# A linear-attention recurrence on one core: converting loads become plain ones, and the stores move to GpSimd's queue

## The chip, the core and the metric

The kernel runs on one core of a Trainium2 chip. The metric is device time in microseconds (us), the median of three runs. A core has five engines that run side by side: PE (TensorE, matrix products), DVE (VectorE), ACT (ScalarE), POOL (GpSimd) and SP (SyncE, which here only issues transfers). Sixteen DMA engines move data between HBM (main memory) and SBUF (the on-chip memory of 128 partitions). PSUM holds the results of PE.

## The reference

For each of 16 batches and each of 256 channels, a recurrence runs over 2048 time steps. It keeps a weighted sum of v (`aa`), the sum of the weights (`bb`) and a running maximum (`pp`) for safe exponentials:

```python
for t in range(seq_len):
    ww = u + k[t]
    qq = max(pp, ww)
    e1, e2 = exp(pp - qq), exp(ww - qq)
    output[t] = (e1 * aa + e2 * v[t]) / (e1 * bb + e2 + 1e-08)
    ww = pp - w + k[t]
    qq = max(ww, k[t])
    e1, e2 = exp(ww - qq), exp(k[t] - qq)
    aa, bb, pp = e1 * aa + e2 * v[t], e1 * bb + e2, qq
```

k, v and the output are float32 of 16 x 2048 x 256, 33.55 MB each.

## The kernel before

Time is cut into 16 chunks of 128 steps (`TC`), and each chunk into four parts of four batches. A part is a slot, numbered n from 0 to 63 (n = 4c + p). In slot n the kernel

- issues the loads of slot n + 6 (`load`), 512 KB of k and 512 KB of v, in rows of 1 KB
- takes exponentials of sums of k that PE made (`exps`, on ScalarE)
- rounds k(n + 2) to PE's format (`round_k`) and v(n + 1) to bf16 (`cast_v`), and multiplies by v (`times_v`), on VectorE
- makes the denominators of slot n - 10 (`den`, `recip`) and the numerators of slot n - 11 (`num`, `mult`), and stores slot n - 11

Between chunks a small chain (`state_...`, spread over slots by `plan`) carries the state: GpSimd and VectorE work on 128 x 32 tiles, and four small transfers (`inject`) put the state into the rows of the next chunk's operands.

Every instruction stands in program order on its engine (`K(...)` keeps it). A transfer is issued by an engine's queue in that order too: one that waits for its data or its buffer holds those behind it.

```python
    kpool = ctx.enter_context(tc.tile_pool(name="kpool", bufs=AHEAD))      # AHEAD = 6
    vpool = ctx.enter_context(tc.tile_pool(name="vpool", bufs=5))
    vbpool = ctx.enter_context(tc.tile_pool(name="vbpool", bufs=4))
    rpool = ctx.enter_context(tc.tile_pool(name="rpool", bufs=6))

    def v_mode(n):                                                         # LAG = 10
        return "dma" if n >= LAG and n % 4 == 3 else "dve"

    def load_v(n, queue=SP):
        if v_mode(n) == "dma":
            VB[n] = vbpool.tile([128, 4, Dm], BF16, tag="vb", name="vb")
            K(POOL.dma_start(out=VB[n], in_=rows_of(v, n)))                # float32 -> bf16 on the way
        else:
            vr_of[n] = vpool.tile([128, 4, Dm], F32, tag="vr", name="vr")
            K(queue.dma_start(out=vr_of[n], in_=rows_of(v, n)))
    # ... cut ...
    def round_k(n):
        # ... cut ...
        K(DVE.tensor_copy(km, kr_of.pop(n)))
    # ... cut ...
    def inject(c):
        # ... cut: cb is copied by VectorE ...
                K(POOL.dma_start(
                    out=EZR[r:r + 1, 2 * q, r0:r0 + 4, :, :].rearrange("o p i (b x) -> o (p i b) x", b=4),
                    in_=cb[x:x + 32, :]))

    def store(n):
        K(SP.dma_start(out=rows_of(out, n), in_=RD.pop(n).rearrange("p i (n d) -> p (i n) d", n=2)))
    # ... cut ...
    for n in range(LAG, NP):                       # NP = 64
        q, qp = n - LAG, n - LAG - 1
        load(n + AHEAD)
        if qp >= 0:
            num(qp, NUMB, 0)
        den(q)
        small_work(n, "nums")
        exps(n)
        small_work(n, "act")
        if qp >= 0:
            mult(qp, NUMB, 0)
        small_work(n, "mid")
        if n + 2 < NP:
            round_k(n + 2)
        if n + 1 < NP:
            cast_v(n + 1)
        # ... cut ...
        recip(q, lambda: small_work(n, "recip"))
        if qp >= 0:
            mult(qp, NUMB, 1)
        small_work(n, "scan")
        if qp >= 0:
            store(qp)
        if n + 1 < NP:
            times_v(n)
            small_work(n, "chain")
            logs(n + 1)
```

Of the kernel before, what the change touches and what calls it, by code (L numbers as in the profile page):

```python
# [7 lines left out]
F32 = mybir.dt.float32  # L8
F32R = mybir.dt.float32r
BF16 = mybir.dt.bfloat16  # L10
ALU = mybir.AluOpType
ACT = mybir.ActivationFunctionType
# [3 lines left out]
def kernel(  # L16
# [9 lines left out]
    K = tc.keep_in_program_order  # L26
    PE, DVE, SC, POOL, SP = nc.tensor, nc.vector, nc.scalar, nc.gpsimd, nc.sync

    B, T, Dm = k.shape
# [4 lines left out]
    NP = 4 * NST  # L34
    RING = 12
    AHEAD = 6
    LAG = 10
# [5 lines left out]
    kpool = ctx.enter_context(tc.tile_pool(name="kpool", bufs=AHEAD))  # L43
    vpool = ctx.enter_context(tc.tile_pool(name="vpool", bufs=5))
    vbpool = ctx.enter_context(tc.tile_pool(name="vbpool", bufs=4))
    rpool = ctx.enter_context(tc.tile_pool(name="rpool", bufs=6))
    small = ctx.enter_context(tc.tile_pool(name="small", bufs=2))
    tiny = ctx.enter_context(tc.tile_pool(name="tiny", bufs=1))
    ps = ctx.enter_context(tc.tile_pool(name="ps", bufs=1, space=bass.MemoryType.PSUM))
# [2 lines left out]
    kr_of, vr_of, VB = {}, {}, {}  # L52

    def v_mode(n):
        return "dma" if n >= LAG and n % 4 == 3 else "dve"

    def rows_of(x, n):
        c, p = divmod(n, 4)
        return x[4 * p:4 * p + 4, c * TC:(c + 1) * TC, :].rearrange("n t d -> t n d")

    def load_k(n, queue=SP):
        kr_of[n] = kpool.tile([128, 4, Dm], F32, tag="kr", name="kr")
        K(queue.dma_start(out=kr_of[n], in_=rows_of(k, n)))

    def load_v(n, queue=SP):
        if v_mode(n) == "dma":
            VB[n] = vbpool.tile([128, 4, Dm], BF16, tag="vb", name="vb")
            K(POOL.dma_start(out=VB[n], in_=rows_of(v, n)))
        else:
            vr_of[n] = vpool.tile([128, 4, Dm], F32, tag="vr", name="vr")  # L70
            K(queue.dma_start(out=vr_of[n], in_=rows_of(v, n)))


    def load(n):
        for x, f in ((n - 1, load_v), (n, load_k)) if n < LAG + AHEAD else ((n, load_k), (n, load_v)):
            if x < NP and (f == load_k or v_mode(x) != "dma"):
                f(x)

# [35 lines left out]
    for n in range(2, AHEAD):  # L116
        load_k(n)
        load_v(n - 1)
# [61 lines left out]
    def round_k(n):  # L180
        km = consts.tile([128, 4, Dm], F32R, tag=f"km{n % 2}", name="km") if n < 2 else KM[n - 2]
        K(DVE.tensor_copy(km, kr_of.pop(n)))  # L182
        KM[n] = km
# [21 lines left out]
    def exps(n):  # L205
        if n < TURNS:
            for q in range(2):
                K(SC.activation(ez(n)[:, q], half(n, q), ACT.Exp))  # L208
        else:
            K(SC.activation(ez(n)[:, 0:2], PS[:, 0:4, :].rearrange("p (q i) x -> p q i x", q=2), ACT.Exp))  # L210

    def cast_v(n):
        mode = v_mode(n)
        if mode == "dma":
            return
        vb = vbpool.tile([128, 4, Dm], BF16, tag="vb", name="vb")
        vr = vr_of.pop(n)
        if mode == "act":
            K(SC.activation(vb, vr, ACT.Copy))
        elif mode == "pool":  # L220
            K(POOL.tensor_copy(vb, vr))
        else:
            K(DVE.tensor_copy(vb, vr))  # L223
        VB[n] = vb

    def times_v(n):
        vb = VB.pop(n).rearrange("p (i n) d -> p i (n d)", i=2)
        K(DVE.tensor_mul(ez(n)[:, 2:4], ez(n)[:, 0:2], vb.unsqueeze(1).broadcast_to([128, 2, 2, D])))  # L228
# [94 lines left out]
    def state_next(c):  # L323
        G, tb = st.pop((c, "G")), st.pop((c, "tb"))
        AB, nxt = AB_of[c % 2], AB_of[(c + 1) % 2]
        y = tiny.tile([128, 2, 32], F32, tag="y", name="y")
        K(POOL.tensor_mul(y, AB[:, :, 1, :], G[:, 1, :].unsqueeze(1).broadcast_to([128, 2, 32])))
        K(POOL.tensor_add(nxt[:, :, 0, :], y, tb[:, :, 1, :]))

        if 4 * c + 11 < NP:  # L330
            load_v(4 * c + 11)


    def turn_back(c):
        t = MISC[:, Dm:Dm + 128]
# [17 lines left out]
    RD = {}  # L353

    def den(n):
        for m, q in (("L", 0), ("Id", 1)):
            for i in range(2):
                K(PE.matmul(DENB[:, i, :], mats[m], ez(n)[:, q, i, :], start=q == 0, stop=q == 1,  # L358
                            skip_group_check=True))
# [9 lines left out]
    def num(n, bank, i):  # L369
        for m, q in (("LN", 2), ("IdN", 3)):  # L370
            K(PE.matmul(bank, mats[m], ez(n)[:, q, i, :], start=q == 2, stop=q == 3, skip_group_check=True))  # L371

    def mult(n, bank, i):
        rd = RD[n]
        K(DVE.tensor_mul(rd[:, i, :], bank, rd[:, i, :]))  # L375

    def store(n):
        K(SP.dma_start(out=rows_of(out, n), in_=RD.pop(n).rearrange("p i (n d) -> p (i n) d", n=2)))

    def last_outputs(n, H):  # L380
        c, p = divmod(n, 4)
# [7 lines left out]
    for c in range(NST):  # L389
        s = 4 * c + 3  # L390
        plan = [(s + 1, "act" if s + 1 < LAG else "recip", copy_sums), (s + 1, "pe", turn),
                (s + 2, "act", state_logs), (s + 2, "mid", state_frames), (s + 2, "scan", state_scan), (s + 2, "scan", state_offsets),
                (s + 3, "recip", state_weights), (s + 3, "chain", state_chain),
                (s + 4, "nums", turn_back), (s + 4, "mid", inject), (s + 4, "mid", state_next)]
        if c == 0:
            plan = [(s + 1, "act", copy_sums), (s + 1, "pe", turn), (s + 2, "act", state_logs),
                    (s + 2, "chain", state_frames), (s + 2, "chain", state_scan), (s + 2, "chain", state_offsets),
                    (s + 3, "act", state_weights), (s + 3, "chain", state_chain),
                    (s + 4, "logs", turn_back), (s + 4, "logs", inject), (s + 4, "round", state_next)]
        if c == 1:  # L400
            plan = [(s + 1, "act", copy_sums), (s + 1, "pe", turn), (s + 2, "act", state_logs),
                    (s + 2, "chain", state_frames), (s + 2, "chain", state_scan), (s + 2, "chain", state_offsets)] + plan[6:]
        if c == NST - 1:
            plan = [(s + 1, "copy", copy_sums), (s + 1, "turn", turn),
                    (s + 1, "post", state_logs), (s + 1, "mid", state_frames), (s + 1, "mid", state_scan), (s + 1, "mid", state_offsets),
                    (s + 2, "post", state_weights), (s + 2, "first", state_chain),
                    (s + 3, "turn", turn_back), (s + 3, "first", inject)]
        for slot, where, f in plan:
            later.setdefault((slot, where), []).append((f, c))

    def small_work(n, where):
        for f, c in later.pop((n, where), []):
            f(c)
# [10 lines left out]
    logs(0)  # L424
    round_k(1)
    cast_v(0)
    for n in range(LAG):

# [19 lines left out]
    for n in range(LAG, NP):  # L448

        q, qp = n - LAG, n - LAG - 1  # L450
        load(n + AHEAD)
        if qp >= 0:
            num(qp, NUMB, 0)
        den(q)
# [13 lines that stand above are left out]
            num(qp, NUMB, 1)  # L468

        sums(n - 1)  # L470
        recip(q, lambda: small_work(n, "recip"))
        if qp >= 0:
            mult(qp, NUMB, 1)
        small_work(n, "scan")
        if qp >= 0:
            store(qp)
        if n + 1 < NP:
            times_v(n)
            small_work(n, "chain")
            logs(n + 1)  # L480
        else:
            den(q + 1)
        small_work(n, "pe")
    sums(NP - 1)
    small_work(NP, "copy")
    late = []
    for n in range(NP, NP + LAG + 1):

        q, qp = n - LAG, n - LAG - 1
        H = PS[:, 2 * (n % 2):2 * (n % 2) + 2, :]  # L490
        for i in range(2):
            num(qp, H[:, i, :], i)
        small_work(n, "turn")
        if q < NP:
            recip(q, lambda: small_work(n, "recip"))
        small_work(n, "post")
        if q + 1 < NP:
            den(q + 1)
        small_work(n, "first")
        if qp == NP - 1:  # L500
            last_outputs(qp, H)
            break
        late.append((qp, H))
        if n != NP + 1:

            for x, bank in late:
                mult(x, bank, slice(0, 2))
                store(x)
            late = []
        small_work(n, "mid")  # L510
    assert not later
# [30 lines left out]
```

## Time and profile before

| | |
|---|---|
| median of 3 runs | 293.66 us (293.6 to 293.93) |
| span of the profiled run | 291.6 us |
| HBM read, written | 67.12 MB, 33.55 MB |
| loads of k, by SP's queue | 64 of 512 KB, 9.0 us from issue to landing |
| loads of v, by SP's queue | 50 of 512 KB, 9.1 us |
| converting loads of v, by POOL's queue | 14 of 256 KB written, 8.5 us |
| stores, by SP's queue | 63 of 512 KB, 8.3 us |
| injects, by POOL's queue | 64 of 8 KB, 5.2 us |

The landing times are medians. Busy time counts the instructions of an engine; an engine that is not busy waits for data, a buffer or another engine. The DMA row of the page cuts the span into 40 slices of 7.3 us and gives the mean busy share of the 16 DMA engines in tenths (9 is 90% or more), and the GB/s row what they wrote. q0 is GpSimd's queue, q1 SyncE's, q10 ScalarE's. In a line of the timeline the first number is the start in us, the second the duration.

### The profile page before, as it was taken

To read this page: it belongs to the slowest core of one execution; us is meant where nothing else is said; L and a number is where in the kernel's file an instruction comes from. 1 tells how busy PE (TensorE), PEld (TensorE's weight loads), DVE (VectorE), ACT (ScalarE), POOL (GpSimd) and SP (SyncE) were. 2 spreads that over 40 slices of the span, in tenths; PEclk is the share of its full clock that TensorE was granted. 3 is DMA by queue.
4 is the path that set the end of the run, shared out by engine and by line. 5 is a ranking of instruction groups with operands and counts; after the bars stand their busy time and mean duration, and the time that the engine had idled before them with its cause. 6 is when DMAs were issued, how large, how long until landed. Compare 5 with 4: busy or idle time off the path is not lost. (4 is left out here: it accounts for less than half of the span.)

```text
span 291.6 us, 4937 instructions
## 1 busy us (share of the span) xinstructions
PE 258.8 (89%) x1662; PEld 120.1 (41%) x1694; DVE 256.4 (88%) x439; ACT 256.6 (88%) x253; POOL 120.4 (41%) x226
## 2 busy tenths in 40 slices
PE   5996998999999999988998999898899989988881
PEld 1433443444443444434443444444344444434330
DVE  4798899999999999999989989897998989886753
ACT  2586589999999999999899999989899998999892
POOL 7000345453544465553534555452455545342200
PEclk9699799999999999999999999999999999999997
DMA  7999999999999999999999999999999999984686
GB/s 228 351 348 349 347 323 329 297 385 332 374 351 360 375 338 382 338 371 336 380 342 370 377 336 378 331 385 334 373 380 336 381 333 382 334 283 153 220 288 216
DMA packets 103521, 97.86 MB, mean 336 GB/s; under 512 B 4156, under 2 KB 103496, under 8 KB 103496
## 3 DMA queue, kind: packets, MB, share of 16 engines
q1 hardware_dynamic: 93752, 93.08, 94.7%
q0 software_dynamic: 9440, 4.20, 10.0%
q10 hardware_dynamic: 304, 0.27, 0.3%
q8 instruction: 13, 0.21, 0.3%
q14 instruction: 12, 0.10, 0.1%
HBM read 67.12 MB, written 33.55 MB: 345 GB/s over the span
## 5 line engine op out<-in xcount | busy, mean ns | idle before, releaser
L210 ACT ACTIVATE EZR<-PS 128x2048 bf16<-128x2048 f32 x54 | 101.3, 1875 | 5.7 <-PE PS L197 4.9
L375 DVE TENSOR_TENSOR rd<-PS,rd 128x512 f32<-128x512 f32 (+1 forms) x118 | 85.9, 730 | 7.8 <-PE PS L371 6.6
L228 DVE TENSOR_TENSOR EZR<-EZR,vb 128x2048 bf16<-128x2048 bf16 x64 | 77.7, 1215 | 2.6 <-ACT EZR L208 1.5
L366 ACT ACTIVATE rd<-rd 128x1024 f32<-128x1024 f32 (+1 forms) x65 | 68.0, 1047 | 1.2
L364 ACT ACTIVATE rd<-PS 128x1024 f32<-128x1024 f32 (+1 forms) x65 | 65.9, 1013 | 1.7 <-PE PS L358 1.6
L348 POOL DMA_DIRECT2D EZR<-cb x64 | 38.2, 602 | 60.8 <-DVE cb L343 49.1
L371 PE MATMUL PS<-EZR,LN 128*128 128x512 bf16 x128 | 48.7, 380 | 13.7 <-DVE rd L375 10.3
L182 DVE CAST km<-kr 128x1024 fp32r<-128x1024 f32 x64 | 45.8, 715 | 11.9 <-DMA kr<-in_k_dram 11.8
L197 PE MATMUL PS<-km,NLE 128*128 128x512 f32 x128 | 47.8, 455 | 2.4 <-DVE km L182 2.4
L371 PE MATMUL PS<-EZR,IdN 128*128 128x512 bf16 x114 | 43.1, 378 | 0.0
L197 PE MATMUL PS<-km,NLZ 128*128 128x512 f32 x128 | 41.4, 406 | 0.0
L358 PE MATMUL PS<-EZR,L 128*128 128x512 bf16 x127 | 37.8, 379 | 1.7 <-ACT rd L364 1.7
L223 DVE CAST vb<-vr 128x1024 bf16<-128x1024 f32 x50 | 35.9, 719 | 0.8 <-DMA vr<-in_v_dram 0.8
L358 PE MATMUL PS<-EZR,Id 128*128 128x512 bf16 x114 | 35.0, 379 | 0.1
L283 POOL TENSOR_TENSOR F<-LL,LL 128x32 f32<-128x32 f32 x13 | 7.9, 604 | 51.1 <-ACT LL L274 51.1
L191 PE MATMUL PS<-WU,CO 32*128 32x512 bf16 x256 | 26.7, 391 | 2.2 <-DVE WU L423 1.7
L208 ACT ACTIVATE EZR<-PS 128x1024 bf16<-128x1024 f32 x20 | 19.4, 1020 | 10.2 <-PE PS L197 10.2
L252 PE MATMUL PS<-EZR,OH 128*32 128x256 bf16 x512 | 26.1, 280 | 2.1
L197 PEld LDWEIGHTS PS<-km,NLZ 128*128 128x128 f32 x128 | 24.7, 193 | 5.8
L197 PEld LDWEIGHTS PS<-km,NLE 128*128 128x128 f32 x128 | 19.4, 191 | 17.4 <-issue 13.8
L371 PEld LDWEIGHTS <-IdN 128*128 128x128 bf16 x128 | 12.5, 97 | 26.7 <-issue 23.9
L296 POOL TENSOR_TENSOR Q<-P,F 128x64 f32<-128x64 f32 x13 | 15.7, 1204 | 12.1 <-DVE P L287 12.1
(72 smaller groups left out, 213.7 us busy)
## 6 DMA issues: line engine op xcount, KB each, us to landing
kr<-in_k_dram SPq DMA_DIRECT2D x64, 512.0 KB, 9.0
out_dram<-rd SPq DMA_DIRECT2D x63, 512.0 KB, 8.3
vr<-in_v_dram SPq DMA_DIRECT2D x50, 512.0 KB, 9.1
vb<-in_v_dram POOLq DMA_DIRECT2D x14, 256.0 KB, 8.5
EZR<-cb POOLq DMA_DIRECT2D x64, 8.0 KB, 5.2
out_dram<-rd SPq DMA_DIRECT2D x2, 128.0 KB, 3.0
out_dram<-rd ACTq DMA_DIRECT2D x2, 128.0 KB, 3.3
wuf<-in_w_dram ACTq DMA_DIRECT2D x1, 8.0 KB
```

Source lines behind the costliest of these rows:

```text
L182: K(DVE.tensor_copy(km, kr_of.pop(n)))
L191: K(PE.matmul(half(n, q)[:, i, :], CO[g:g + 32, :], WU[g:g + 32, :].unsqueeze(1).broadcast_to([32, 2, Dm]), start=True, stop=False, tile_p ...
L197: K(PE.matmul(half(n, q)[:, i, :], (NLE, NLZ)[q], km[:, i, :], start=False, stop=True, skip_group_check=True))
L210: K(SC.activation(ez(n)[:, 0:2], PS[:, 0:4, :].rearrange("p (q i) x -> p q i x", q=2), ACT.Exp))
L223: K(DVE.tensor_copy(vb, vr))
L228: K(DVE.tensor_mul(ez(n)[:, 2:4], ez(n)[:, 0:2], vb.unsqueeze(1).broadcast_to([128, 2, 2, D])))
L348: K(POOL.dma_start(out=EZR[r:r + 1, 2 * q, r0:r0 + 4, :, :].rearrange("o p i (b x) -> o (p i b) x", b=4), in_=cb[x:x + 32, :]))
L358: K(PE.matmul(DENB[:, i, :], mats[m], ez(n)[:, q, i, :], start=q == 0, stop=q == 1, skip_group_check=True))
L364: K(SC.activation(rd[:, i, :], DENB[:, i, :], ACT.Ln, scale=RS))
L366: K(SC.activation(rd[:, i, :], rd[:, i, :], ACT.Exp, scale=-1.0))
L371: K(PE.matmul(bank, mats[m], ez(n)[:, q, i, :], start=q == 2, stop=q == 3, skip_group_check=True))
L375: K(DVE.tensor_mul(rd[:, i, :], bank, rd[:, i, :]))
```

## The change

No load converts any more: all of v comes as float32 by SP's queue, and GpSimd rounds one v in four to bf16 (and v 5, 6 and 7 in the first slots, which VectorE rounded). The stores go by GpSimd's queue, two slots after the slot that made their data, so that GpSimd needn't wait for them; eight result buffers instead of six hold the data for longer. In the tail the stores stay on SP's queue. In the first chunk, the state's `state_chain` stands behind the rounding of k in VectorE's order. The purpose is to keep waiting stores out of the loads' queue and the conversion out of the transfers.

```diff
-    rpool = ctx.enter_context(tc.tile_pool(name="rpool", bufs=6))
+    rpool = ctx.enter_context(tc.tile_pool(name="rpool", bufs=8))
# ... cut ...
     def v_mode(n):
-        return "dma" if n >= LAG and n % 4 == 3 else "dve"
+        return "pool" if n in (5, 6, 7) or n >= LAG and n % 4 == 3 else "dve"
# ... cut ...
     def load_v(n, queue=SP):
-        if v_mode(n) == "dma":
-            VB[n] = vbpool.tile([128, 4, Dm], BF16, tag="vb", name="vb")
-            K(POOL.dma_start(out=VB[n], in_=rows_of(v, n)))
-        else:
-            vr_of[n] = vpool.tile([128, 4, Dm], F32, tag="vr", name="vr")
-            K(queue.dma_start(out=vr_of[n], in_=rows_of(v, n)))
+        vr_of[n] = vpool.tile([128, 4, Dm], F32, tag="vr", name="vr")
+        K(queue.dma_start(out=vr_of[n], in_=rows_of(v, n)))
 
     def load(n):
-        for x, f in ((n - 1, load_v), (n, load_k)) if n < LAG + AHEAD else ((n, load_k), (n, load_v)):
-            if x < NP and (f == load_k or v_mode(x) != "dma"):
-                f(x)
+        if n - 1 < NP:
+            load_v(n - 1)
+        if n < NP:
+            load_k(n)
# ... cut: cast_v loses its "dma" and "act" branches; state_next loses its load_v(4 * c + 11) ...
-    def store(n):
-        K(SP.dma_start(out=rows_of(out, n), in_=RD.pop(n).rearrange("p i (n d) -> p (i n) d", n=2)))
+    def store(n, queue=POOL):
+        K(queue.dma_start(out=rows_of(out, n), in_=RD.pop(n).rearrange("p i (n d) -> p (i n) d", n=2)))
# ... cut: plan of chunk 0 ...
-                    (s + 3, "act", state_weights), (s + 3, "chain", state_chain),
+                    (s + 3, "act", state_weights), (s + 3, "round", state_chain),
# ... cut: for n in range(LAG, NP) ...
         load(n + AHEAD)
+
+        if qp >= 2:
+            store(qp - 2)
# ... cut ...
         small_work(n, "scan")
-        if qp >= 0:
-            store(qp)
# ... cut: after the loop ...
     late = []
+    store(NP - LAG - 3)
+    store(NP - LAG - 2)
# ... cut: in the tail ...
                 mult(x, bank, slice(0, 2))
-                store(x)
+                store(x, SP)
```

More of the change, by code (lines that the diff above doesn't have):

```diff
@@ L213, in cast_v @@
         mode = v_mode(n)
-        if mode == "dma":
-            return
         vb = vbpool.tile([128, 4, Dm], BF16, tag="vb", name="vb")
         vr = vr_of.pop(n)
-        if mode == "act":
-            K(SC.activation(vb, vr, ACT.Copy))
-        elif mode == "pool":
+        if mode == "pool":
             K(POOL.tensor_copy(vb, vr))
@@ L328, in state_next @@
         K(POOL.tensor_add(nxt[:, :, 0, :], y, tb[:, :, 1, :]))
-        if 4 * c + 11 < NP:
-            load_v(4 * c + 11)
     def turn_back(c):
```

## The prediction

> **What bounds the kernel now.** I read the page first, from busy shares to the DMA line.
>
> ```profile
> PE 258.8 (89%) x1662; PEld 120.1 (41%) x1694; DVE 256.4 (88%) x439; ACT 256.6 (88%) x253; POOL 120.4 (41%) x226
> ...
> DMA  7999999999999999999999999999999999984686
> GB/s 228 351 348 349 347 323 329 297 385 332 374 351 360 375 338 382 338 371 336 380 342 370 377 336 378 331 385 334 373 380 336 381 333 382 334 283 153 220 288 216
> ...
> q1 hardware_dynamic: 93752, 93.08, 94.7%
> q0 software_dynamic: 9440, 4.20, 10.0%
> ```
>
> Three compute engines are equally full, and the DMA engines are full from about 7 us to 255 us. Only the first slice and the last five have slack. The end is therefore: the last load lands (the last k is issued at 244.3 us and rounded at 252.7 us), then a tail of some 39 us of compute drains ten slots of outputs. The chain that ended last begins only at 271.2 us and lies in that tail (PE, ACT and DVE in turn), which the change leaves alone. So the question is how fast the slots before 257 us go.
>
> To see whether DMA or compute sets the slot, I took the starts of ScalarE's large exponential (one a slot; four slots are a chunk of 128 time steps, called round below) from its timeline, early and late:
>
> ```profile
> 60.44 1.85 ACT L210 ACTIVATE EZR<-PS 128x2048 bf16<-128x2048 f32 x1
> ...
> 76.26 1.88 ACT L210 ACTIVATE EZR<-PS 128x2048 bf16<-128x2048 f32 x1
> ...
> 225.75 1.85 ACT L210 ACTIVATE EZR<-PS 128x2048 bf16<-128x2048 f32 x1
> ...
> 242.57 1.86 ACT L210 ACTIVATE EZR<-PS 128x2048 bf16<-128x2048 f32 x1
> ```
>
> Early a round takes 15.82 us, late 16.82 us, with the same instructions. Early the buffers are ahead and compute sets the pace (ScalarE 69.3 us busy of the 70 from 50 to 120 us). Late it doesn't: the waits from 120 to 257 us name k's transfer.
>
> ```profile
> DVE km L182 <- DMA kr<-in_k_dram: 10.7, 24, 1.2
> ...
> ACT G L304 <- POOL A L299: 4.6, 8, 0.9
> ```
>
> So the late stage is DMA-bound by 1.0 us a round, over (257-120)/16.8 = 8.2 rounds: **8 us is the most** that faster transfers can give before compute takes over.
>
> Then what slows the transfers. The table by stretches shows the rate (its last two columns are the DMA engines' share and GB/s written):
>
> ```profile
> 10.00:38.00 28.00, 25.06 (x163) 11.67 (x165) 24.97 (x49) 18.49 (x23) 4.49 (x8) 0.84 1.09 348
> ...
> 151.00:154.00 3.00, 2.94 (x21) 1.30 (x21) 2.68 (x5) 2.96 (x5) 1.69 (x3) 1.00 1.24 271
> 155.00:163.00 8.00, 7.22 (x50) 3.27 (x51) 7.56 (x15) 7.04 (x8) 4.37 (x9) 1.00 1.08 384
> ```
>
> Loads alone (10 to 38 us) run at 348 GB/s, loads and stores mixed at 384 with no converting load in flight. In 151 to 154 us one of the 14 converting loads runs. It writes half the bytes it reads, so 271 understates the work: the packet records count 484 converting packets in those 3 us, each with 512 B not counted, which adds 83 GB/s: 354 against 384. Its packets take 59 ns each (median), and those of the other queue beside it 58, where plain ones take 46.
>
> **What the Trainium skill says.** "DMA: Bandwidth & Descriptors", section "Issuing engines are not separate DMA queues": all queues run on the same 16 engines, and another issuing engine saves only issue time. The trace agrees that issue is not the limit: SyncE's first issues take 0.40 to 0.51 us, and 1.3 us only once the queue has filled, which is back-pressure. The same page, "SWDGE vs HWDGE vs iDMA": converting needs GpSimd's software queue, whose descriptors GpSimd writes to SBUF rings; VectorE can lock it out of that. Here the 14 converting loads cost GpSimd 0.82 us each and land 8.5 us after issue, against 9.1 for SyncE's v loads: no sign of starvation, at one load a round. "SBUF — State Buffer", "Who interferes with whom": GpSimd and VectorE share a port pair, held for the whole instruction, when VectorE is in a two-port mode or (against a GpSimd op that reads SBUF) has two SBUF inputs. The trace shows something like it: GpSimd's 128x64 tensor op takes 0.33 us at 145.97 us and 1.20 us at 153.64 us. "GPSIMD Engine Reference", "4.1 Engine selection": a one-input op there is roughly at line rate; by 3.1 of that page, 1.03 cycles an element, I estimate 1024 x 1.03 / 1.2 GHz = 0.9 us for rounding one v. No run here shows it yet.
>
> **The change, part by part.** Instruction order on PE and ScalarE is unchanged; VectorE loses three casts.
>
> 1. *No converting loads.* 14 go. Packets stay equal (512 of 1 KB read each), so the gain is the rate: 3 us x (1 - 354/384) = 0.23 us each, and somewhat more at the edges of each stretch: 14 x 0.3 = **-4 us** of DMA time, nearly all before 257 us.
>
> 2. *Stores two slots later, on their own queue.* Today SyncE holds 46 stores ahead of the last k load. In the new order 45 (numbers 0 to 44) are programmed up to that slot. One store of 0.52 MB at 384 GB/s is **-1.4 us** before the last load. The stores move into the tail, whose last six slices have some 15 us of free DMA time. Loads no longer stand behind a store that waits for data, but SyncE's queue has some 9 us of work in flight (issue to landing), so these waits (23.8 us on SyncE from 120 to 250 us) cost little now. Eight rd buffers cover the longer life.
>
> 3. *The mixture of the two queues.* Per round 4096 load packets and 2048 store packets. While a store runs, loads and stores alternate packet by packet; if that goes at 384 GB/s, 4096 packets take 10.9 us. The other 2048 are loads alone, at 348 to 384: 6.0 to 5.5 us. Sum 16.4 to 16.9 us a round. Today all 6144 packets at 384 GB/s would be 16.4 us; with 0.3 for the converting load, 0.1 of the 16.8 is left for the four small injects. So after: 16.5 to 17.0, against 16.5 today once part 1 is taken off. I choose a point near the fast end, +0.1 a round, because load bursts between two stores run today at some 370 packets a us (379 GB/s, packet records): over 8 to 12 rounds **+1 us**.
>
> 4. *GpSimd.* Per round +4 stores x 0.82, -1 converting load x 0.82, +1 cast of 0.9 to 2 us: +3.4 to 4.5 us on some 7.5 us busy. It has room. The cast of v(4c+3) is programmed a slot before its product needs it, after the state chain's offsets; the injects move back by 2 to 4 us and stand behind a store in the queue, with about three slots (12 us) between inject and first use, against 5.2 us to landing. So no new wait on ScalarE's weights or on the outputs is expected.
>
> 5. *VectorE.* In the late stage its count is unchanged (that v was never its work). Where compute sets the pace it is 98% busy too (19.54 of 20 us from 60 to 80 us), and GpSimd's cast may block it for part of 0.9 us a round: I take 0.3 us x 4 compute-bound rounds = **+1 us**.
>
> 6. *Start.* v(5), v(6), v(7) leave VectorE (3 x 0.6 us between starts), and the first chain no longer holds the rounding of k(8): at 31.15 us VectorE waits 0.5 us for it. The first ten slots go up to 2 us faster, but the DMA engines are full from 7 us on, so this only empties buffers sooner: **0 to -0.5 us**.
>
> Sum: -4 - 1.4 + 1 + 1 - 0.3 = -3.7 us: 293.66 - 3.7 = **290.0 us**. The limit of 8 us is not reached.
>
> **Rivals.**
>
> *Two queues cost an exchange each packet.* If the 59 and 58 ns beside converting loads come from alternating with the software queue and not from converting, all stores bring it: 4096 packets of each round at 354 instead of 384 GB/s, +0.9 us a round, 12 rounds: +11 us, and without part 1's gain about +13: 303 to 305 us. For it: the neighbours slow down too, stores as well as loads. Against it: around the small injects of the same queue (164 to 166 us) the neighbours stay at 46 ns, and in the tail two hardware queues alternate store packets at 46 to 48 ns. I give it one in five.
>
> *Compute takes over at once.* If the mixed queues keep 384 GB/s throughout, DMA needs 16.4 us a round and VectorE and ScalarE 15.8 to 16.1. The late rounds shrink by 0.6 to 0.9 us: -5 to -7 us, 286.5 to 288.5 us. For it: the gap late is all k's transfer. Against it: loads alone ran at 348. Three in ten.
>
> *GpSimd becomes a link.* Store issues or a cast stretched by VectorE delay the state offsets, for which ScalarE already waits 0.5 to 0.6 us a round. One us more a round is +12 us. The order puts stores where GpSimd idles (4.0 us before its state frames, 3.5 us before the injects), so one in ten; and the injects' slack hides most.
>
> **Range and chances.** The middle case gives 288 to 292, the compute-bound one 286 to 288.5, the exchange and GpSimd cases 297 to 305. Eighty per cent lies in 285 to 299. Two per cent is 287.8 and 299.5: faster 0.28, same 0.54, slower 0.18.
>
> **What would show it.** In the profile after: q0 near 27 to 29 MB with plain 1 KB packets; no 59 ns packets if converting was their cause, or 59 on both queues if it was the exchange (then GB/s in the middle slices falls to about 350). VectorE's waits for k fall below 5 us if part 1 holds. Late rounds between 15.9 and 16.7 us by the exponential's starts; above 16.9 the prediction is wrong. GpSimd's cast near 1 us, and waits on the state weights for GpSimd as today. The tail from the last rounding of k to the end stays near 39 us; if it grows by over 2 us, the moved stores were not free.

## The result: 301.12 us, and the profile after

| | us, median of 4 runs each, same chip | ratio to before, 95% interval |
|---|---|---|
| before | 293.68 (293.6 to 293.93) | |
| after | 301.12 (300.63 to 302.12) | 1.0256 (1.0227 to 1.0286) |

The change costs 2.6%, outside the range of the prediction. First the page of the kernel after: busy shares, the rows by slice, the packets by size, the two queues, and the transfers with their median us from issue to landing.

```profile
PE 262.8 (88%) x1694; PEld 119.9 (40%) x1694; DVE 268.0 (90%) x436; ACT 255.5 (85%) x253; POOL 166.5 (56%) x282
...
GB/s 220 352 348 350 348 332 345 341 386 367 365 364 373 371 376 376 372 376 359 370 368 377 378 371 380 366 365 367 369 371 371 376 372 370 229 140 155 255 300 217
DMA packets 83170, 101.54 MB, mean 340 GB/s; under 512 B 4156, under 2 KB 76360, under 8 KB 83144
...
q1 hardware_dynamic: 73160, 72.63, 74.4%
q0 software_dynamic: 9680, 28.32, 25.0%
...
kr<-in_k_dram SPq DMA_DIRECT2D x64, 512.0 KB, 11.5
vr<-in_v_dram SPq DMA_DIRECT2D x64, 512.0 KB, 11.3
out_dram<-rd POOLq DMA_DIRECT2D x53, 512.0 KB, 7.4
```

VectorE is busier by 11.6 us although it has three instructions fewer: something holds it. The packets between 2 KB and 8 KB are 83144 - 76360 = 6784. That is 27.8 MB at 4096 B each, which is the 53 stores of GpSimd's queue: they do not travel in packets of 1 KB. k lands 11.5 us after its issue instead of 9.0, yet the waits for it from 120 to 257 us are fewer (before, 10.7 us in 24 waits), and ScalarE's exponential has a new one (before, 3.0 us, at most 0.4):

```profile
ACT EZR L207 <- PE PS L194: 7.6, 8, 1.1
...
DVE km L179 <- DMA kr<-in_k_dram: 2.6, 2, 1.3
```

The starts of ScalarE's large exponential divide the loss. Slot 10 starts 0.35 us earlier than before (39.66 against 40.01 us), slots 10 to 63 take 225.86 instead of 219.16 us (+6.70), and from slot 63 to the end 33.40 instead of 32.42 us (+0.98); together +7.3 us of span. The rounds of four slots from slot 12 on, in us:

```
before 16.07 15.80 15.82 15.77 16.45 17.10 16.76 16.79 16.82 17.47 16.77 16.81
after  17.04 16.67 16.66 16.67 18.92 16.84 16.63 16.68 16.67 18.91 16.75 16.67
```

The early rounds have lost the pace of 15.8, and two rounds stand out at 18.9. Two mechanisms can be read from the trace.

**GpSimd's rounding stands where VectorE's chain is due.** The timeline of after in one round (start, duration):

```profile
161.82 1.30 DVE L221 TENSOR_TENSOR EZR<-EZR,vb 128x2048 bf16<-128x2048 bf16 x1
...
161.98 0.85 POOL L368 DMA_DIRECT2D out_dram<-rd  x1
...
162.84 1.18 POOL L214 CAST vb<-vr 128x1024 bf16<-128x1024 f32 x1
...
163.04 1.05 DVE L306 TENSOR_TENSOR x<-AB,G 128x64 f32<-128x64 f32 x1
163.21 1.88 ACT L207 ACTIVATE EZR<-PS 128x2048 bf16<-128x2048 f32 x1
...
168.01 1.88 ACT L207 ACTIVATE EZR<-PS 128x2048 bf16<-128x2048 f32 x1 [0.91 <-PE PS L194]
```

The rounding runs from 162.84 to 164.02 us. VectorE's `x<-AB,G`, the first link of the state chain, with two inputs in SBUF, is due at 163.04 and ends at 164.09, 0.07 us behind the rounding. Its durations by tile (least, median, most, in ns), of before and of after:

```profile
L313 DVE TENSOR_TENSOR x<-AB,G x15: 209/216/248, 44.2 to 268.1; 128x64 f32<-128x64 f32 x15
```

```profile
L306 DVE TENSOR_TENSOR x<-AB,G x15: 211/1052/1054, 44.5 to 275.5; 128x64 f32<-128x64 f32 x15
```

The 0.84 us go down the chain: PE, which turns the state, starts on it later, and the next exponential starts 0.91 us late (the bracket at 168.01). The slot with n % 4 = 3 takes 4.80 to 4.83 us in nine rounds of twelve, where before had 3.93 to 3.98 us in its early rounds.

**The stores' packets and the loads' packets do not mix evenly.** Windows of after, once with a store of GpSimd's queue in flight, once without (the last three columns are PE's clock, the DMA share, and the GB/s written):

```profile
142.00:143.50 1.50, 1.50 (x8) 0.62 (x8) 1.49 (x2) 1.50 (x2) 1.42 (x2) 1.00 1.03 400
145.50:147.50 2.00, 1.93 (x9) 0.68 (x7) 1.97 (x4) 2.00 (x3) 2.00 (x3) 1.00 1.09 343
155.50:156.50 1.00, 1.00 (x6) 0.49 (x5) 0.75 (x2) 1.00 (x1) 0.00 (x0) 1.00 1.10 331
157.50:160.00 2.50, 2.50 (x20) 1.24 (x20) 2.50 (x5) 2.47 (x3) 1.89 (x3) 1.00 1.04 398
```

The packet records of after, counted in steps of 0.5 us from 70 to 245 us and sorted by the rate of the stores in each step:

```
stores GB/s   steps  stores  loads  together  mean ns of a 1 KB load packet
none            110       0    338       338  51.9
under 100        76      37    323       359  48.7
100 to 150       24     127    254       380  47.3
150 to 250       48     201    185       386  47.2
over 250         92     304     94       399  46.7
```

While a store is in full flow it takes three quarters of the rate and the loads get 94 GB/s; in nearly a third of the steps the loads are alone, at 338. The mean over this stretch is 371 GB/s (window). The Trainium skill has on the page "DMA: Bandwidth & Descriptors", section "Queues, rings and completion order", that each DMA engine goes round the queue rows that have work and drains a whole packet before it switches. The trace agrees in size: one 4096 B packet (164 ns, median) and one of 1 KB (46.7 ns) in turn on 16 engines would give 5120 B x 16 / 211 ns = 388 GB/s, four fifths of it stores, which is an estimate; the records have 399, with 76% stores.

When a late k and GpSimd's work fall together, VectorE loses more. Timeline of after at the first of the two long rounds:

```profile
125.84 0.85 POOL L368 DMA_DIRECT2D out_dram<-rd  x1
126.02 2.29 DVE L179 CAST km<-kr 128x1024 fp32r<-128x1024 f32 x1 [1.21 <-DMA kr<-in_k_dram]
...
126.69 1.05 POOL L214 CAST vb<-vr 128x1024 bf16<-128x1024 f32 x1
```

This k took 14.3 us to land (the chain that ended last). Its rounding then took 2.29 instead of 0.69 us, and ended 0.57 us after GpSimd's rounding. The same pair stretches VectorE's product at 264.17 us to 2.73 us, across the start of slot 63, from which the tail is counted: that is most likely the +0.98 of the tail. In all three places a store's issue, the rounding and another issue stand in a row on GpSimd. Experiment 9, below, has the stores without the rounding; the durations of k's rounding, of after and of 9:

```profile
L179 DVE CAST km<-kr x64: 677/685/2285, 4.9 to 259.0; 128x1024 fp32r<-128x1024 f32 x64
```

```profile
L179 DVE CAST km<-kr x64: 679/684/1067, 4.9 to 259.0; 128x1024 fp32r<-128x1024 f32 x64
```

Its longest, 1.07 us, stands beside two issues in a row. So issues alone go with some 0.4 us at most in 9, and the long ones need GpSimd's rounding.

### The profile page after: what moved, and what is told of

It is laid out like the page before. It is cut to its first block, busy times and chain, and to the rows that moved or that the text cites. A ratio compares the mean times of both kernels' runs of the same rounds, so it can differ in the third digit from the quotient of the medians.

```text
span 298.9 us, 4976 instructions
## 1 busy us (share of the span) xinstructions
PE 262.8 (88%) x1694; PEld 119.9 (40%) x1694; DVE 268.0 (90%) x436; ACT 255.5 (85%) x253; POOL 166.5 (56%) x282
## 2 busy tenths in 40 slices
DMA packets 83170, 101.54 MB, mean 340 GB/s; under 512 B 4156, under 2 KB 76360, under 8 KB 83144
## 3 DMA queue, kind: packets, MB, share of 16 engines
q0 software_dynamic: 9680, 28.32, 25.0%
## 4 chain that ended last, share of the span: by engine, by line
PE 35%; DVE 24%; DMA 21%; issue 8%; ACT 6%; POOL 4%; SPq 0%; DVEq 0%; POOLq 0%; ACTq 0%
DMA kr<-in_k_dram 13%; PE PS L361 10%; DVE EZR L221 10%; PE PS L194 9%; PE PS L348 7%; DVE rd L365 6%; DMA out_dram<-rd 6%; PE PS L245 3%; PE PS L188 3%; ACT rd L354 3%; DVE x L306 2%; DVE km L179 2%; DMA wuf<-in_u_dram 1%; DVE vb L216 1%; PE PS L262 1%
## 5 line engine op out<-in xcount | busy, mean ns | idle before, releaser
L221 DVE TENSOR_TENSOR EZR<-EZR,vb 128x2048 bf16<-128x2048 bf16 x64 | 79.9, 1248 | 1.4 <-ACT EZR L205 1.3
L338 POOL DMA_DIRECT2D EZR<-cb x64 | 38.9, 614 | 35.7 <-DVE cb L333 27.2
L179 DVE CAST km<-kr 128x1024 fp32r<-128x1024 f32 x64 | 48.0, 749 | 4.7 <-DMA kr<-in_k_dram 4.2
L194 PE MATMUL PS<-km,NLE 128*128 128x512 f32 x128 | 46.7, 446 | 4.3 <-DVE km L179 4.3
L361 PE MATMUL PS<-EZR,IdN 128*128 128x512 bf16 x128 | 49.0, 383 | 0.0
L368 POOL DMA_DIRECT2D out_dram<-rd x53 | 45.0, 851 | 6.8 <-ACT EZR L207 4.5
L348 PE MATMUL PS<-EZR,L 128*128 128x512 bf16 x128 | 39.0, 387 | 1.6 <-ACT rd L354 1.5
L194 PE MATMUL PS<-km,NLZ 128*128 128x512 f32 x128 | 40.1, 395 | 0.0
L348 PE MATMUL PS<-EZR,Id 128*128 128x512 bf16 x128 | 39.0, 387 | 0.0
L214 POOL CAST vb<-vr 128x1024 bf16<-128x1024 f32 x17 | 20.3, 1195 | 16.6 <-DMA vr<-in_v_dram 16.6
L194 PEld LDWEIGHTS PS<-km,NLZ 128*128 128x128 f32 x128 | 24.0, 188 | 5.6
## 6 DMA issues: line engine op xcount, KB each, us to landing
kr<-in_k_dram SPq DMA_DIRECT2D x64, 512.0 KB, 11.5
```

Of the source, the lines that this page charges most:

```text
L194: K(PE.matmul(half(n, q)[:, i, :], (NLE, NLZ)[q], km[:, i, :], start=False, stop=True, skip_group_check=True))
L338: K(POOL.dma_start(out=EZR[r:r + 1, 2 * q, r0:r0 + 4, :, :].rearrange("o p i (b x) -> o (p i b) x", b=4), in_=cb[x:x + 32, :]))
L368: K(queue.dma_start(out=rows_of(out, n), in_=RD.pop(n).rearrange("p i (n d) -> p (i n) d", n=2)))
```

## Experiments

The theories: **rounding**, that GpSimd's conversion of v delays VectorE's chain; **queue**, that stores on GpSimd's queue make the transfers slower; and as rivals that the two slots of delay or the eight buffers cost the time, or the new start. The change also issues each v's load one slot later than before did, from slot 16 on (`load` in the diff). All kernels below but 2 and 11 have this order, so it cannot make the differences among them; no run isolates it. Each ratio is to runs of the kernel before on the same chip.

**1. The conversion of every fourth v left out** from slot 11 on; the product takes a constant buffer instead, so a quarter of v does not enter the output.

```diff
+        if mode == "pool" and n >= LAG:
+            VB[n] = VBX          # constant, 0.5
+            return
```

> The changed kernel without GpSimd's rounding of every fourth v from slot 11 on (its float32 load still comes; the product takes a constant buffer, so this work is left out). Theory A, the port: GpSimd's rounding holds VectorE's first chain operation (1.05 us instead of 0.21), which moves ScalarE's next exponential by 0.94 us a round of four slots. Then rounds go from 16.67 to 15.8-16.0 us and the time to 288-291 us. Theory B, the transfers: GpSimd's 4 KB store packets starve the loads (landing 11.5 us instead of 9.0). Then nothing but the two late k transfers matters and the time stays at 298-301 us.

Measured: 318.69 us (313.51 to 320.18), against 293.74. The run tests something else. With no reader of these v's left, the next load into their buffer had to wait until the earlier load had landed. SyncE's waits:

```profile
SPq L67 <- DMA vr<-in_v_dram: 103.5, 12, 12.1
```

Twelve waits of up to 12.1 us stop the whole load queue. It says nothing about the rounding; experiment 5 repeats the question with a reader kept.

**2. Stores alone:** before, with the stores of the change (GpSimd's queue, two slots late, eight buffers); the converting loads stay.

```diff
-    rpool = ctx.enter_context(tc.tile_pool(name="rpool", bufs=6))
+    rpool = ctx.enter_context(tc.tile_pool(name="rpool", bufs=8))
-    def store(n):
+    def store(n, queue=POOL):
+        if qp >= 2:
+            store(qp - 2)        # after load(n + AHEAD)
-            store(qp)            # after small_work(n, "scan")
```

> The kernel before with one part of the change: stores by GpSimd's queue two slots behind, eight result buffers; the converting loads stay and GpSimd rounds nothing. Theory A: no long GpSimd read stands beside the chain, and the stores' own issues cost little: 285-290 us, better than both kernels. Theory B: the stores' packets delay the loads as in the changed kernel: 298-302 us.

Measured: 297.54 us, 1.014 (1.0117 to 1.0163). VectorE's waits for k from 120 to 257 us are as long as before, in fewer and longer pieces:

```profile
DVE km L182 <- DMA kr<-in_k_dram: 10.7, 10, 2.4
```

The rounds are 15.8 early and 16.2 to 18.5 later. The stores alone cost more than half of the loss.

**3. Loads and rounding alone:** after, with the stores on SyncE in their old place and six buffers.

```diff
-    rpool = ctx.enter_context(tc.tile_pool(name="rpool", bufs=8))
+    rpool = ctx.enter_context(tc.tile_pool(name="rpool", bufs=6))
-    def store(n, queue=POOL):
+    def store(n, queue=SP):
-        if qp >= 2:
-            store(qp - 2)
+        if qp >= 0:
+            store(qp)            # after small_work(n, "scan")
```

> The changed kernel with its stores back on SyncE's queue in their old place and six result buffers; no load converts and GpSimd rounds one v in four. Theory A: the block of the chain stays, rounds of 16.6-16.8 us and more where the transfers are late too: 298-303 us. Theory B: with the old stores the loss goes: 290-294 us.

Measured: 295.74 us, 1.0076 (1.0049 to 1.0103). VectorE has no waits for k among its longer ones from 120 to 257 us; what is left is the exponential's wait of after, once a round:

```profile
ACT EZR L207 <- PE PS L194: 7.3, 8, 1.1
```

`x<-AB,G` has a median of 1050 ns, and the rounds are 16.63 to 16.68 but for two: the chain sets the pace from the first round to the last. Both parts of the change cost time; alone they come to 1.4% and 0.76%, of the 2.6% together.

**4. Rounding a slot earlier:** after, with GpSimd's rounding of a v two slots ahead of its product, behind the store at the start of the slot.

```diff
+        if LAG + 1 < n + 2 < NP and v_mode(n + 2) == "pool":
+            cast_v(n + 2)        # after store(qp - 2)
-            cast_v(n + 1)
+            if n == LAG or v_mode(n + 1) != "pool":
+                cast_v(n + 1)
```

> The changed kernel with GpSimd's rounding of every fourth v two slots ahead of its product instead of one, where GpSimd stands idle ahead of the state's frames (some 3 us). Theory A: the rounding meets VectorE's rounding of k instead of the chain; it may still cost up to 0.3 us a round, so rounds of 15.9-16.2 us and 289-293 us; if v lands too late there, GpSimd's chain waits and it is 294-300 us. Theory B: no change, 299-302 us.

Measured: 300.64 us, 1.0237 (1.0217 to 1.0257): not told apart from after. Yet the lock is gone, by the durations of the tile:

```profile
L306 DVE TENSOR_TENSOR x<-AB,G x15: 210/211/225, 46.3 to 275.1; 128x64 f32<-128x64 f32 x15
```

The second to fourth rounds fall from 16.67 to 16.22 to 16.29, the late ones rise to between 16.7 and 17.7: freed of the rounding beside the chain, the kernel runs into v's transfers. GpSimd itself now waits for v, whose lead the earlier place has shortened (27.2 us in 8 waits from 120 to 257 us), and what follows it in the state's work waits too (VectorE's scan for GpSimd 7.4 us, ScalarE's weights 8.6 us), while VectorE waits for k only 1.3 us.

**5. GpSimd rounds 32 of 1024 columns.** As in 1 the product takes a constant buffer, but a reader of the loaded v stays.

```diff
+        if mode == "pool" and n >= LAG:
+            K(POOL.tensor_copy(VBX[:, :, 0:8], vr[:, :, 0:8]))
+            VB[n] = VBX
+            return
```

> The changed kernel, but GpSimd rounds only 32 of the 1024 columns of every fourth v (the product takes a constant buffer; the rest is left out), so each load is read and its buffer comes free as in the changed kernel. Theory A alone (the port): rounds of 15.8-16.0 us throughout, 288-291 us. Theory C (the queues: 4 KB store packets take most of the engines while they last, 395 GB/s in all, and leave stretches of loads alone at 338 GB/s, so transfers need 17.1 us a round): rounds start at 15.85 and turn to about 17.1 with waits for k, 296-299 us. Then A and C hold together, and one hides the other.

Measured: 299.51 us, 1.0187 (1.0168 to 1.0206).

```profile
L310 DVE TENSOR_TENSOR x<-AB,G x15: 209/216/228, 45.3 to 274.5; 128x64 f32<-128x64 f32 x15
```

The first rounds are 15.90 and 15.84, the pace of before, so the rounding was what held the chain, and 0.84 us a round is its size there. But with hardly any rounding at all 1.9% of loss are left: from the third round on it is 15.85 to 18.45, with k's transfer named again. The queue is the larger part.

**6. Stores on SyncE, rounding a slot earlier** (3 with the edit of 4).

> Stores on SyncE's queue in their old place, no load converts, GpSimd rounds every fourth v two slots ahead of its product, away from the chain. Theories A and C: transfers at 375 GB/s or more (16.4-16.8 us a round at most), the chain not blocked: rounds of 16.2-16.5 us, 289-293 us, better than both kernels; if v lands too late for it, 293-296 us.

Measured: 295.55 us, 1.0054 (1.0037 to 1.0071), the same as experiment 3 within the intervals. Here the rounding waits for its v, and passes the wait on (60 to 257 us):

```profile
POOL vb L214 <- DMA vr<-in_v_dram: 57.2, 12, 6.2
```

**7. Stores on SyncE, VectorE rounds every v from slot 8 on** (3 with one more edit).

```diff
-        return "pool" if n in (5, 6, 7) or n >= LAG and n % 4 == 3 else "dve"
+        return "pool" if n in (5, 6, 7) else "dve"
```

> Stores on SyncE's queue, no load converts, VectorE rounds every v from slot 8 on. VectorE gets 0.6 us more a round of four slots. Theory A: no block; rounds of 16.4-16.5 us, 290-294 us, that is at or below the rounding on GpSimd (295.7), for the same bytes. If the loss by the rounding on GpSimd were not the port, this should be 0.6 us x 13 rounds slower than that: 300 us and more.

Measured: 292.99 us, 0.9969 (0.9956 to 0.9983): a little faster than before, and the fastest version of all. The rate is even from the first store to the last load, and waits for k have all but gone (60 to 257 us):

```profile
GB/s 216 352 348 350 348 330 349 341 378 375 381 378 375 377 375 381 374 379 374 380 376 381 376 380 383 378 381 377 377 378 370 375 378 371 376 245 152 224 284 216
```

```profile
DVE km L179 <- DMA kr<-in_k_dram: 1.2, 3, 0.8
```

The rounds are 16.23 to 16.34 until the last two, which take 17.48 and 16.97. VectorE's added rounding of some 0.6 us has raised the pace of compute from 15.8 to 16.24; before drove faster early and waited for k late. So the two come out nearly equal.

**8. Stores on SyncE, but two slots late and with eight buffers** (after with `queue=SP` in `store`, nothing else).

> The changed kernel with its stores on SyncE's queue, still two slots late and with eight result buffers. Theory C (the queue and its packets matter, not the delay): as with the stores in their old place, 16.65 us a round and no late k, 294.5-297 us. If the delay of the stores were the cause of the late k: 299-302 us.

Measured: 296.14 us, 1.0072 (1.0044 to 1.01), against 295.74 in 3. Delay and buffers cost nothing that can be seen; the queue does. Both kernels are paced by the chain at 16.65, so a small saving by the delay would not show either.

**9. and 10. VectorE rounds, stores on GpSimd's queue, or on ScalarE's** (after with the edit of 7; in 10 also `queue=SC`). 10 asks if any second queue costs this.

> The changed kernel with every v from slot 8 on rounded by VectorE: all work done, stores by GpSimd's queue two slots late. With the same roundings and stores on SyncE's queue it was 292.99 us. Theory C (the queue alone costs, without any block by a rounding): transfers limit late rounds to about 17.1 us, 295.5-299.5 us. If the queue cost only in company with GpSimd's rounding: 292-294 us.

> As the last, but the stores go by ScalarE's queue, still two slots late. Theory C by packets (GpSimd's store packets hold 4 KB each and so take four parts of the engines' turns in five): here packets of 1 KB alternate one to one, stretches with stores run at some 380 GB/s with 190 for the stores, loads alone still at 338; rounds of 16.3-16.9 us, 292.5-296.5 us. Theory C by queue (any second queue lets loads run alone and costs the same): 17.1 us late, 296-300 us. ScalarE's own time for the issues can add to either; its waits will show it.

Measured: 299.23 us, 1.0179 (1.0159 to 1.0198), and 298.39 us, 1.0156 (1.0141 to 1.0171). The windows of 9 and 10 over 70 to 245 us:

```profile
70.00:245.00 175.00, 161.81 (x1073) 75.51 (x1072) 165.65 (x268) 163.14 (x157) 114.66 (x174) 1.00 1.07 368
```

```profile
70.00:245.00 175.00, 162.48 (x1077) 77.00 (x1076) 163.68 (x269) 163.26 (x158) 81.90 (x134) 0.99 1.09 379
```

The same window of 7:

```profile
70.00:245.00 175.00, 166.09 (x1105) 76.93 (x1103) 168.10 (x279) 168.45 (x161) 87.68 (x137) 1.00 1.09 377
```

With VectorE rounding, GpSimd's queue gives 368 GB/s, ScalarE's 379, SyncE's 377. In 9 eight of the twelve rounds take 16.24 to 16.65 us, one 17.04, and the loss stands in three of 18.14 to 18.79, where k comes 1.3 to 1.5 us late. ScalarE's stores go as 1 KB packets, and by the packet records the most common steps have 191 GB/s of stores beside 189 of loads. This is the even exchange that the prediction assumed. Experiment 10 is slow for another reason: the issue of a store waits and holds ScalarE's arithmetic behind it. Its timeline:

```profile
74.27 1.06 ACT L356 ACTIVATE rd<-rd 128x1024 f32<-128x1024 f32 x1
78.34 0.38 ACTq L368 DMA_DIRECT2D out_dram<-rd  x1
78.76 1.88 ACT L207 ACTIVATE EZR<-PS 128x2048 bf16<-128x2048 f32 x1 [3.43 <-DVE rd L365]
```

The exponential stood 3.43 us behind an issue; why that issue waited isn't shown. Two early rounds take 17.2 and 20.3 us; the six after them 16.2 to 16.5. In time, then, 10 does not say whether any second queue costs this; by its rate, a second queue as such does not slow the transfers.

What it is in GpSimd's queue stays in part open, for 9 and 10 differ in more than the size of the packets. GpSimd issues its stores behind its state work, and in 9 mostly two at once, where ScalarE issues one in each slot:

```profile
133.49 1.77 POOL L368 DMA_DIRECT2D out_dram<-rd  x2
142.45 1.64 POOL L368 DMA_DIRECT2D out_dram<-rd  x2
```

By the packet records, counted in steps of 0.25 us, the stretches without a store last 3.6 us on average in 9 and 1.1 us in 10. The loads alone in them run at 344 GB/s in 9, and in 10 at 374, down to 349 where 2 us or more have passed since the last store. So 338 is not the rate of lone loads everywhere, and no run holds the spacing of the stores fixed while the packets change.

**11. The new start alone** (before, with v 5 to 7 on GpSimd and `state_chain` behind the rounding of k).

```diff
-        return "dma" if n >= LAG and n % 4 == 3 else "dve"
+        return "pool" if n in (5, 6, 7) else "dma" if n >= LAG and n % 4 == 3 else "dve"
-                    (s + 3, "act", state_weights), (s + 3, "chain", state_chain),
+                    (s + 3, "act", state_weights), (s + 3, "round", state_chain),
```

> The kernel before with only the change's start: v 5, 6 and 7 rounded by GpSimd, the first chain behind the rounding of k. All theories: the transfers are full from 7 us on, so 293.0-294.0 us; first large exponential at 39-40 us in the place of 40.0.

Measured: 293.8 us, 1.0005 (0.9994 to 1.0015). The start gives and costs nothing that can be seen. In the profile of 11 the first large exponential starts at 41.71 us and not at 39 to 40; among the profiles of these kernels, 12 aside, it starts between 39.6 and 42.0 us without a pattern in the edits, so the 0.35 us by which after starts earlier is not shown to be a gain either.

**12. GpSimd's queue for loads:** 7, with v 5 to 12 loaded by GpSimd's queue, to see loads alone in 4 KB packets.

```diff
-        K(queue.dma_start(out=vr_of[n], in_=rows_of(v, n)))
+        queue = POOL if 5 <= n <= 12 else SP
+        K(queue.dma_start(out=vr_of[n], in_=rows_of(v, n)))
```

> The best so far (stores on SyncE's queue, no converting loads, VectorE rounds, 292.99 us) with v 5 to 12 loaded by GpSimd's queue, before any store is in flight. If GpSimd's packets of 4 KB are what runs fast (stretches with many of them at 395 GB/s), the first 50 us of loads go above the 348 GB/s of today and the time falls to 290.5-292.5 us. If reading HBM alone is the limit whatever the packet, the stretch stays at 340-350 GB/s and the time at 292.5-294.5 us, or above if k waits behind the larger packets.

Measured: 294.93 us, 1.0036 (1.002 to 1.0053). The windows of after and of 12 while only loads run:

```profile
10.00:38.00 28.00, 21.99 (x164) 10.26 (x164) 24.38 (x46) 18.77 (x24) 8.89 (x11) 1.00 1.09 349
```

```profile
10.00:38.00 28.00, 22.14 (x131) 10.84 (x130) 21.60 (x41) 14.83 (x18) 10.61 (x14) 0.80 1.08 349
```

The same 349 GB/s, with 805 packets of 4096 B, a third of the bytes, in this stretch of 12; in the steps of 0.5 us in which they carry over 200 GB/s, all loads together run at 353. So large packets are not slow in themselves. That stores in such packets cost by pushing loads aside and leaving them alone later fits the table of after, but is argued. The loss of 12 itself lies at its start: slot 10 begins at 45.38 us, in 7 at 41.49.

**Summary.** Four runs make a square:

| stores / every fourth v | VectorE rounds | GpSimd rounds |
|---|---|---|
| SyncE's queue | 292.99 (7) | 295.74 (3) |
| GpSimd's queue | 299.23 (9) | 301.12 (after) |

From before to 7 it is -0.7 us, GpSimd's rounding adds 2.75, and then GpSimd's queue 5.4: the 7.4 of the change. In the other order the queue costs 6.2 and the rounding 1.9. The lower row also has the two slots of delay and the eight buffers, for which 8 showed no cost on SyncE's queue.

## Why the prediction was wrong

By the square: steps 1 and 6 were to give -4.3 us and, with VectorE's rounding in it, gave -0.7; step 5 was to cost 1 and cost 2.75; steps 2 and 3 were to give -0.4 together and cost 5.4. The steps in turn:

**Step 3 failed, and it is the largest error.** It put +1 us on the mixture: loads and stores alternating packet by packet at 384 GB/s, and lone loads at 348 to 384 with a point near the fast end. Measured: +5.4 to +6.2 us, with whatever step 2 gave in it. Two of its assumptions fell. The packets are not equal: GpSimd's queue sends 4096 B where SyncE's sends 1 KB, so stores and loads share 304 to 94 and not 1 to 1. And lone loads run at 338, below the slow end. The rate from 70 to 245 us is 368 in 9 against 377 in 7, 2.4% less; over the 210 us or so in which loads and stores are both under way I estimate 5 us from it. The fast end was taken from load bursts between stores on one queue (379 GB/s), which did not carry over to stores on GpSimd's; with ScalarE's (10) the lone loads do run at 374. What slows them behind GpSimd's stores, the packets of 4096 B or the wider and uneven spacing, isn't shown.

**Step 5 failed in size and in reach.** It took 0.3 us in 4 rounds as VectorE's cost of GpSimd's cast, +1 us. The cast holds one instruction by 0.84 us, the first link of the state chain, which is due just when the cast runs; and it does so in nearly every round. On SyncE's queue, where the transfers keep up, the chain sets the pace to the end (16.65 against 16.24 in 7), which is +2.75. On GpSimd's queue a part is hidden under the late transfers, +1.9. The page of the Trainium skill that the prediction cites, "SBUF — State Buffer", section "Who interferes with whom", names this very case (a VectorE instruction with two SBUF inputs against a GpSimd one that reads SBUF), and the trace agrees: 0.21 us became 1.05. The error was to spread it as a share of time, and not to look at which instruction would be under it.

**Step 1 was right in kind, and did not become time.** Its -4 us were the slower converting loads, and k's waits do disappear (10.7 us in 24 waits before; none of note in 3, 1.2 us from 60 to 257 us in 7). But the rounding has to be done by someone: on VectorE it raises the pace to 16.24, on GpSimd to 16.65. With VectorE, -0.7 us remain. Nor did the transfers gain much in all: before writes 359 GB/s from 70 to 245 us, and with the 0.26 MB that each of some 10.6 converting loads (one a round of 16.5 us) reads and does not write, 375, against 377 in 7. The step had taken the 384 of one 8 us stretch for the rate of plain loads and stores, and over the long window that is 377 (7) and 378 (3). What plain loads would give at a pace of 15.8 was not run: no kernel here has plain loads, stores on SyncE and no added rounding.

**Step 2** expected -1.4 us from the later stores. Between 3 and 8 no gain is seen (+0.4, intervals overlap).

**Step 4** held as far as order goes: GpSimd had room, its cast took 1.05 and 1.18 us in the two places shown (median of all 1.19, least 1.04, against the 0.9 estimated), and ScalarE's wait for the state offsets (4.6 us before) is not among the longer waits any more. **Step 6** held within the noise: 0 to -0.5 us was expected, and 11 measured +0.1 (-0.2 to +0.4).

**The rivals.** The exchange at each packet would have made 303 to 305 us, near the result, but not by its mechanism: load packets take 47 to 52 ns, not 59, and two queues with 1 KB packets (10) run at 379 GB/s. GpSimd as a link came true by a way that was not named: its rounding holds VectorE, and not its issues or late offsets ScalarE. Compute did set the pace of most rounds, but at the 16.67 us of the held chain and not at the 15.8 to 16.1 of that rival.

**The signs named in advance.** q0 holds 28.32 MB, as expected, but not in 1 KB packets. The waits for k fell below 5 us, which was to confirm part 1, while the time rose: the wait had only moved. Rounds above 16.9 us were to refute the prediction, and two of 18.9 did. The tail from the last rounding of k grew by 1.0 us (its start is at 259.0 instead of 252.7 us), within the 2 us allowed.

## What to carry to other kernels

A second queue is no free lane: before moving a steady stream to it, look at its packet size against the other's and at how evenly its engine can issue. Here the larger packets took three quarters of the rate while they lasted, and the loads alone afterwards ran at 338 GB/s. Before giving GpSimd a conversion, find the two-input VectorE instruction that will be due in the same microsecond; if it heads a chain that sets the pace, its whole delay is paid, as in 3. When a wait disappears and the time does not fall, compare the pace of the early rounds with the late ones, for that shows which limit has taken its place.

## What the runs showed that was not expected

- The 512 KB stores go as 4096 B packets (164 ns) from GpSimd's queue and as 1 KB packets from SyncE's and ScalarE's, from the same buffer to the same rows.
- Loads alone run at 348 to 353 GB/s at the start with either size of packet (before, 12); with stores above 100 GB/s beside them the records of after have 380 to 399 in all. Loads alone run at 344 between GpSimd's stores (9) and at 374 between ScalarE's (10).
- A load whose data nobody reads is dear: the next load into its buffer waited for it to land (1, up to 12.1 us each).
- Stores on ScalarE's queue can stop its arithmetic for 3.4 us (10), though the transfers ran at 379 GB/s, against 377 with SyncE's.
